# Attention for one query row: normalising at the output, score matmuls one head behind, and loads cut and ordered anew

## The chip, the cores and the metric

The kernel runs on one core of a Trainium2 chip. The metric is device microseconds of one execution. The core has five engines that run side by side and wait for each other through semaphores: TensorE (PE; its weight loads are shown as PEld), VectorE (DVE), ScalarE (ACT), GpSimd (POOL) and SyncE (SP). DMA transfers are issued by an engine's queue and carried by 16 DMA engines.

## The reference

```
batch, n_heads, kv_len, head_dim = 4, 8, 1024, 64
scores = scale * np.matmul(q, k.transpose(0, 1, 3, 2))
scores_max = np.max(scores, axis=-1, keepdims=True)
attn = np.exp(scores - scores_max) / (np.sum(np.exp(scores - scores_max), axis=-1, keepdims=True) + 1e-8)
return np.matmul(attn, v).astype(np.float32)
```

There are 32 heads (batch times heads), each with one query row of 64, and K and V of 1024 rows of 64, all float32. K and V are 8.4 MB each, so 16.8 MB are read for an output of 8 KB.

## The kernel before

**Layout.** The 1024 rows of a head are split as 128 partitions by C = 8 rows each (`p c`). [...] There are NG = 4 loads for K and 4 for V, each of HG = 8 heads: 2 MB read, 1 MB written. All eight stand first in POOL's order; the constants (`ident`, `identb`, `Wq`, `G`, `G2`; L81 to L101) are made by POOL after them. The two loads of q stand first on SP and on ACT (L72, L73).

**Scores.** q is transposed once on PE (L105) and copied by DVE into `Wq` (L110, L114), a matrix of zeros in which head h has a 64-column block with only columns 2h and 2h+1 filled. For each head, four PE transposes (L128, two rows of `c` at a time) turn K into `kt_ps` in PSUM, ACT (even heads, L135) or DVE (odd heads, L137) copies it to `kt_sb`, and a matmul (L138) with that head's block of `Wq` adds into the one accumulator `S_ps` of 64 x 512: rows 2h and 2h+1 hold the scores of head h. `kt_ps` and `kt_sb` have three buffers each.

**Softmax.** DVE takes the maximum of each row of `S_ps` (L147), ACT makes `E` = exp(scale * S - scale * m) with its row sums (L151) and `c_r` = exp(scale * m) (L159). Each head has two rows, each with its own maximum; `c_r` brings them to a common scale. `den` = `c_r` * rowsum (L160); a matmul with `G` adds the two rows of a head (L165), DVE inverts (L167), a matmul with `G2` spreads the result to both rows (L169), and `d_r` = `c_r` / Z stands on the diagonal of `dinv` (L172). Four matmuls (L177) transpose and scale `E` by it at once; DVE and ACT copy the results into `Pt` (L185, L187).

**Output.** For each head, eight matmuls (L196) of one column of `Pt` against 128 x 64 of V add into a 64-wide piece of one of four PSUM banks `avo`, eight heads to a bank. DVE and ACT copy the banks in turn into `ores` (L206, L210), and SP stores it (L211).

**What sets the order.** The program is written engine by engine by a framework that adds the semaphore waits and sets the order of each engine's instructions by its own estimate; on PE some transposes of later heads stand ahead of a head's score matmul. Pools of buffers decide when a tile may be written again. Loads issued by POOL have eight completion semaphores, used in turn.

Of the kernel before, what the change touches and what calls it, by code (L numbers as in the profile page):

```python
# [9 lines left out]

FP32 = mybir.dt.float32
BF16 = mybir.dt.bfloat16
ACT = mybir.ActivationFunctionType
ALU = mybir.AluOpType


def _strided_cols(ap: bass.AP, row0: int, nrows: int, col0: int, step: int, count: int):
    base = ap[row0 : row0 + nrows, col0 : col0 + 1]
    return bass.AP(
        tensor=base.tensor,  # L20
        offset=base.offset,
        ap=[[base.ap[0][0], nrows], [step, count]],
    )


@with_exitstack
def kernel(
# [7 lines left out]
    nc = tc.nc  # L35

    B, H, L, D = k.shape
    BH = B * H
# [4 lines left out]
    R = 2 * BH  # L43
    SCALE = 1.0 / math.sqrt(D)

    NG = 4
    HG = BH // NG

    big = ctx.enter_context(tc.tile_pool(name="big", bufs=1))
    consts = ctx.enter_context(tc.tile_pool(name="consts", bufs=1))  # L50
    small = ctx.enter_context(tc.tile_pool(name="small", bufs=1))
    ktp = ctx.enter_context(tc.tile_pool(name="ktp", bufs=3))

    k_view = k.rearrange("b h (p c) d -> p (b h) c d", c=C)
    v_view = v.rearrange("b h (p c) d -> p (b h) c d", c=C)
    q_view = q.rearrange("b h o d -> (b h) (o d)")
    out_view = out.rearrange("b h o d -> o (b h d)")

    K_bf = big.tile([P, BH, C, D], BF16, name="K_bf")
    V_bf = big.tile([P, BH, C, D], BF16, name="V_bf")  # L60
    q32 = big.tile([BH, 2, D], FP32, name="q32")
    Wq = big.tile([P, 2176], BF16, name="Wq")
    E = big.tile([R, 512], BF16, name="E")
    Pt = big.tile([P, JJ, R], BF16, name="Pt")
    ores = big.tile([1, BH * D], FP32, name="ores")

    ident = consts.tile([P, P], FP32, name="ident")
    identb = consts.tile([P, P], BF16, name="identb")
    G = consts.tile([R, BH], FP32, name="G")
    G2 = consts.tile([BH, R], FP32, name="G2")  # L70

    nc.sync.dma_start(out=q32[:, 0, :], in_=q_view)  # L72
    nc.scalar.dma_start(out=q32[:, 1, :], in_=q_view)  # L73
    for g in range(NG):
        hs = slice(g * HG, (g + 1) * HG)
        nc.gpsimd.dma_start(out=K_bf[:, hs, :, :], in_=k_view[:, hs, :, :])  # L76
    for g in range(NG):
        hs = slice(g * HG, (g + 1) * HG)
        nc.gpsimd.dma_start(out=V_bf[:, hs, :, :], in_=v_view[:, hs, :, :])  # L79

    make_identity(nc, ident[:])  # L81
    make_identity(nc, identb[:])
    nc.gpsimd.memset(Wq[:], 0.0)  # L83
    nc.gpsimd.memset(G[:], 1.0)
    nc.gpsimd.affine_select(
        out=G[:], in_=G[:], compare_op=ALU.is_ge, fill=0.0, base=0,
        channel_multiplier=1, pattern=[[-2, BH]],
    )
    nc.gpsimd.affine_select(
        out=G[:], in_=G[:], compare_op=ALU.is_ge, fill=0.0, base=1,  # L90
        channel_multiplier=-1, pattern=[[2, BH]],
    )
    nc.gpsimd.memset(G2[:], 1.0)
    nc.gpsimd.affine_select(
        out=G2[:], in_=G2[:], compare_op=ALU.is_ge, fill=0.0, base=0,
        channel_multiplier=-2, pattern=[[1, R]],
    )
    nc.gpsimd.affine_select(
        out=G2[:], in_=G2[:], compare_op=ALU.is_ge, fill=0.0, base=1,
        channel_multiplier=2, pattern=[[-1, R]],  # L100
    )  # L101

    with tc.tile_pool(name="qps", bufs=1, space=bass.MemoryType.PSUM) as qps:
        qT_ps = qps.tile([P, BH], FP32, name="qT_ps")
        nc.tensor.transpose(  # L105
            out=qT_ps[:],
            in_=q32[:].rearrange("h t d -> h (t d)"),
            identity=ident[0:BH, 0:BH],
        )
        nc.vector.tensor_copy(  # L110
            out=_strided_cols(Wq, 0, 64, 0, 66, BH),
            in_=qT_ps[0:64, :],
        )
        nc.vector.tensor_copy(  # L114
            out=_strided_cols(Wq, 64, 64, 1, 66, BH),
            in_=qT_ps[64:128, :],
        )

    c_r = small.tile([R, 1], FP32, name="c_r")
    den = small.tile([R, 1], FP32, name="den")  # L120
    with tc.tile_pool(name="ps1", bufs=1, space=bass.MemoryType.PSUM) as ps1, tc.tile_pool(
        name="ps_kt", bufs=3, space=bass.MemoryType.PSUM
    ) as ps_kt:
        S_ps = ps1.tile([R, 512], FP32, name="S_ps")
        for h in range(BH):
            kt_ps = ps_kt.tile([P, 512], BF16, name="kt_ps")
            for jj in range(JJ):
                nc.tensor.transpose(  # L128
                    out=kt_ps[:, 128 * jj : 128 * (jj + 1)],
                    in_=K_bf[:, h, 2 * jj : 2 * jj + 2, :],  # L130
                    identity=identb[:],
                )
            kt_sb = ktp.tile([P, 512], BF16, name="kt_sb")
            if h % 2 == 0:
                nc.scalar.copy(out=kt_sb[:], in_=kt_ps[:])  # L135
            else:
                nc.vector.tensor_copy(out=kt_sb[:], in_=kt_ps[:])  # L137
            nc.tensor.matmul(  # L138
                out=S_ps[:],
                lhsT=Wq[:, 64 * h : 64 * h + 64],  # L140
                rhs=kt_sb[:],
                start=(h == 0),
                stop=(h == BH - 1),
            )

        m = small.tile([R, 1], FP32, name="m")
        nc.vector.reduce_max(out=m[:], in_=S_ps[:], axis=mybir.AxisListType.X)  # L147
        negm = small.tile([R, 1], FP32, name="negm")
        nc.vector.tensor_scalar_mul(out=negm[:], in0=m[:], scalar1=-SCALE)
        rowsum = small.tile([R, 1], FP32, name="rowsum")  # L150
        nc.scalar.activation(  # L151
            out=E[:],
            in_=S_ps[:],
            func=ACT.Exp,
            bias=negm[:],
            scale=SCALE,
            accum_out=rowsum[:],
        )
    nc.scalar.activation(out=c_r[:], in_=m[:], func=ACT.Exp, scale=SCALE)  # L159
    nc.vector.tensor_mul(out=den[:], in0=c_r[:], in1=rowsum[:])  # L160

    d_r = small.tile([R, 1], FP32, name="d_r")
    with tc.tile_pool(name="ps_fix", bufs=1, space=bass.MemoryType.PSUM) as ps_fix:
        Z_ps = ps_fix.tile([BH, 1], FP32, name="Z_ps")
        nc.tensor.matmul(out=Z_ps[:], lhsT=G[:], rhs=den[:], start=True, stop=True)  # L165
        zr = small.tile([BH, 1], FP32, name="zr")
        nc.vector.reciprocal(out=zr[:], in_=Z_ps[:])  # L167
        zinv_ps = ps_fix.tile([R, 1], FP32, name="zinv_ps")
        nc.tensor.matmul(out=zinv_ps[:], lhsT=G2[:], rhs=zr[:], start=True, stop=True)  # L169
        nc.vector.tensor_mul(out=d_r[:], in0=c_r[:], in1=zinv_ps[:])  # L170
    dinv = big.tile([R, R], BF16, name="dinv")
    nc.vector.tensor_scalar_mul(out=dinv[:], in0=identb[0:R, 0:R], scalar1=d_r[:])  # L172

    with tc.tile_pool(name="ps_pt", bufs=2, space=bass.MemoryType.PSUM) as ps_pt:
        for jj in range(JJ):
            pt_ps = ps_pt.tile([P, R], FP32, name="pt_ps")
            nc.tensor.matmul(  # L177
                out=pt_ps[:],
                lhsT=E[0:R, 128 * jj : 128 * (jj + 1)],
                rhs=dinv[:],  # L180
                start=True,
                stop=True,
            )
            if jj % 2 == 0:
                nc.vector.tensor_copy(out=Pt[:, jj, :], in_=pt_ps[:])  # L185
            else:
                nc.scalar.copy(out=Pt[:, jj, :], in_=pt_ps[:])  # L187

    with tc.tile_pool(name="ps_av", bufs=1, space=bass.MemoryType.PSUM) as ps_av:
        avo = [ps_av.tile([1, 512], FP32, name=f"avo{bnk}") for bnk in range(4)]  # L190
        for h in range(BH):
            bnk = h // 8
            col = D * (h % 8)
            for c in range(C):
                t, jj = c % 2, c // 2
                nc.tensor.matmul(  # L196
                    out=avo[bnk][0:1, col : col + D],
                    lhsT=Pt[:, jj, 2 * h + t : 2 * h + t + 1],
                    rhs=V_bf[:, h, c, :],
                    start=(c == 0),  # L200
                    stop=(c == C - 1),
                )

        for bnk in range(4):
            if bnk % 2 == 0:
                nc.vector.tensor_copy(  # L206
                    out=ores[0:1, 512 * bnk : 512 * (bnk + 1)], in_=avo[bnk][:]
                )
            else:
                nc.scalar.copy(out=ores[0:1, 512 * bnk : 512 * (bnk + 1)], in_=avo[bnk][:])  # L210
    nc.sync.dma_start(out=out_view, in_=ores[:])  # L211


# [28 lines left out]
```

## Time and profile before

| | us |
|---|---|
| median of six runs | 54.53 (53.97 to 54.75) |
| profiled execution, in all | 54.5 |
| its span | 52.8 |
| first score transposes start | 11.72 |
| last score matmul starts | 34.54 |
| first `avo` matmul starts | 39.52 |
| last V load lands | 47.85 |
| output store issued | 50.55 |

The span runs from the first to the last instruction in the profile; 1.7 us lie around it. Busy shares of the span:

```profile
PE 31.4 (60%) x425; PEld 20.8 (39%) x425; DVE 10.6 (20%) x28; ACT 12.7 (24%) x24; POOL 11.0 (21%) x23
...
PE   0000000219998988988988988720449999937800
...
DVE  0000000003333233243243243162330050004000
ACT  0900000004408138138138137007030000300120
POOL 1999999992000000000000000000000000000000
PEclk9999999999999999999999999995555599999999
```

Each digit is the busy share, in tenths, of one of 40 equal slices of 1.32 us; the last row is the clock granted to TensorE in tenths of full speed.

### The profile page before, as it was taken

The numbers are of one execution on the slowest core, as the hardware profiler recorded it, in microseconds if no ns is written. First come the engines' busy times: TensorE is split into PE (matmuls) and PEld (weight loads), VectorE is DVE, ScalarE is ACT, GpSimd is POOL, SyncE is SP. The second block draws the span as 40 slices with busy tenths as digits, with TensorE's granted clock in tenths as the row PEclk, the third lists the DMA queues.
The fourth block names the chain that finished last, engine by engine and source line by source line (L and its number), as shares of the span: only waits on it lengthen the run. The fifth ranks groups of instructions, "written<-read, shape, count | busy, mean of one in ns | idle before, by whom it ended". The sixth has DMA issues, their size and how long they took to land.

```text
span 52.8 us, 1014 instructions
## 1 busy us (share of the span) xinstructions
PE 31.4 (60%) x425; PEld 20.8 (39%) x425; DVE 10.6 (20%) x28; ACT 12.7 (24%) x24; POOL 11.0 (21%) x23
## 2 busy tenths in 40 slices
PE   0000000219998988988988988720449999937800
PEld 0000000118524625625625525300329999837700
DVE  0000000003333233243243243162330050004000
ACT  0900000004408138138138137007030000300120
POOL 1999999992000000000000000000000000000000
PEclk9999999999999999999999999995555599999999
DMA  0049999999999999999999999999999999810000
GB/s 0 13 29 134 173 194 204 153 150 206 203 206 208 206 208 206 206 208 210 204 209 209 206 205 209 206 206 208 206 210 206 205 210 215 133 31 12 0 6 0
DMA packets 8421, 8.46 MB, mean 160 GB/s; under 512 B 225, under 2 KB 8417, under 8 KB 8417
## 3 DMA queue, kind: packets, MB, share of 16 engines
q0 software_dynamic: 8320, 8.39, 98.1%
q8 instruction: 3, 0.05, 0.3%
q1 hardware_dynamic: 50, 0.02, 0.1%
q10 hardware_dynamic: 48, 0.01, 0.1%
HBM read 16.79 MB, written 0.01 MB: 318 GB/s over the span
## 4 chain that ended last, share of the span: by engine, by line
DMA 76%; POOL 11%; PE 4%; issue 2%; ACT 1%; POOLq 0%
DMA V_bf<-in_v_dram 76%; POOL K_bf L76 6%; POOL V_bf L79 5%; PE avo_422 L196 4%; ACT ores L210 1%; POOLq L226 0%
## 5 line engine op out<-in xcount | busy, mean ns | idle before, releaser
L135 ACT COPY kt_sb<-kt_ps 128x512 bf16<-128x512 bf16 x16 | 8.9, 588 | 21.6 <-PE kt_ps L128 21.6
L128 PE MATMUL kt_ps<-identb,K_bf 128*128 128x128 bf16 x128 | 11.8, 232 | 2.3 <-DMA K_bf<-in_k_dram 2.2
L138 PE MATMUL S_ps<-kt_sb,Wq 128*64 128x512 bf16 x32 | 11.1, 405 | 2.3 <-ACT kt_sb L135 1.1
L137 DVE COPY kt_sb<-kt_ps 128x512 bf16<-128x512 bf16 x16 | 6.8, 425 | 27.2 <-PE kt_ps L128 26.3
L128 PEld LDWEIGHTS <-K_bf 128*128 128x128 bf16 x128 | 7.9, 103 | 10.0 <-issue 7.7
L196 PEld LDWEIGHTS <-Pt 128*1 128x1 bf16 x256 | 8.9, 90 | 1.9 <-issue 1.4
L105 PE MATMUL qT_ps<-ident,q_69 32*128 32x32 f32 x1 | 0.3, 311 | 9.2 <-POOL ident masks.py:199 9.2
L138 PEld LDWEIGHTS <-Wq 128*64 128x64 bf16 x32 | 3.1, 111 | 3.6 <-issue 1.5
L76 POOL DMA_DIRECT2D K_bf<-in_k_dram x4 | 3.7, 928 | 0.8 <-POOLq L226 0.8
L105 PEld LDWEIGHTS qT_ps<-ident,q_69 32*128 32x128 f32 x1 | 0.2, 178 | 9.2 <-POOL ident masks.py:199 9.2
L79 POOL DMA_DIRECT2D V_bf<-in_v_dram x4 | 3.5, 922 | 0.0
L196 PE MATMUL avo_419<-V_bf,Pt 128*1 128x64 bf16 x64 | 3.3, 232 | 0.3 <-ACT Pt L187 0.3
L196 PE MATMUL avo_421<-V_bf,Pt 128*1 128x64 bf16 x64 | 2.2, 193 | 0.7 <-issue 0.7
L196 PE MATMUL avo_422<-V_bf,Pt 128*1 128x64 bf16 x64 | 2.0, 193 | 0.5 <-DMA V_bf<-in_v_dram 0.5
L196 PE MATMUL avo_420<-V_bf,Pt 128*1 128x64 bf16 x64 | 2.0, 193 | 0.0
L83 POOL MEMSET Wq<- 128x2176 bf16 x1 | 2.0, 1971 | 0.0
L210 ACT COPY ores<-avo_420 1x512 f32<-1x512 f32 x1 | 0.6, 576 | 5.3 <-PE avo_420 L196 5.3
L210 ACT COPY ores<-avo_422 1x512 f32<-1x512 f32 x1 | 0.6, 575 | 4.6 <-PE avo_422 L196 4.6
L135 ACT ACT_TABLE_LOAD x1 | 1.3, 1283 | 1.3 <-PEq L226 1.3
L206 DVE COPY ores<-avo_421 1x512 f32<-1x512 f32 x1 | 0.7, 678 | 3.9 <-PE avo_421 L196 3.9
L165 PE MATMUL Z_ps<-den,G 64*32 64x1 f32 x2 | 0.2, 185 | 2.0 <-DVE den L160 2.0
L206 DVE COPY ores<-avo_419 1x512 f32<-1x512 f32 x1 | 0.7, 678 | 3.5 <-PE avo_419 L196 3.5
(32 smaller groups left out, 8.7 us busy)
## 6 DMA issues: line engine op xcount, KB each, us to landing
K_bf<-in_k_dram POOLq DMA_DIRECT2D x4, 1024.0 KB, 16.7
V_bf<-in_v_dram POOLq DMA_DIRECT2D x4, 1024.0 KB, 33.4
q_69<-in_q_dram ACTq DMA_DIRECT2D x1, 8.0 KB, 1.8
q_69<-in_q_dram SPq DMA_DIRECT2D x1, 8.0 KB, 1.7
out_dram<-ores SPq DMA_DIRECT2D x1, 8.0 KB
```

The lines of the kernel that those rows point to most:

```text
L76: nc.gpsimd.dma_start(out=K_bf[:, hs, :, :], in_=k_view[:, hs, :, :])
L79: nc.gpsimd.dma_start(out=V_bf[:, hs, :, :], in_=v_view[:, hs, :, :])
L83: nc.gpsimd.memset(Wq[:], 0.0)
L105: nc.tensor.transpose(out=qT_ps[:], in_=q32[:].rearrange("h t d -> h (t d)"), identity=ident[0:BH, 0:BH],)
L128: nc.tensor.transpose(out=kt_ps[:, 128 * jj : 128 * (jj + 1)], in_=K_bf[:, h, 2 * jj : 2 * jj + 2, :], identity=identb[:],)
L135: nc.scalar.copy(out=kt_sb[:], in_=kt_ps[:])
L137: nc.vector.tensor_copy(out=kt_sb[:], in_=kt_ps[:])
L138: nc.tensor.matmul(out=S_ps[:], lhsT=Wq[:, 64 * h : 64 * h + 64], rhs=kt_sb[:], start=(h == 0), stop=(h == BH - 1),)
L165: nc.tensor.matmul(out=Z_ps[:], lhsT=G[:], rhs=den[:], start=True, stop=True)
L196: nc.tensor.matmul(out=avo[bnk][0:1, col : col + D], lhsT=Pt[:, jj, 2 * h + t : 2 * h + t + 1], rhs=V_bf[:, h, c, :], start=(c == 0), stop ...
L206: nc.vector.tensor_copy(out=ores[0:1, 512 * bnk : 512 * (bnk + 1)], in_=avo[bnk][:])
L210: nc.scalar.copy(out=ores[0:1, 512 * bnk : 512 * (bnk + 1)], in_=avo[bnk][:])
```

## The change

K is loaded in eight groups of four heads; V in five groups of 8, 8, 6, 6 and 4 heads. On POOL the first K group is issued before the constants, the second and third between the selects of `G`, and the others after them. The fills with constants move from POOL to DVE, so that POOL keeps the selects only; `G2` is gone. `kt_ps` and `kt_sb` have four buffers, and the loop emits the score matmul of a head after the transposes of the next. `c_r` is made ahead of `E`, and `dinv` holds `c_r` alone, so that the transposed weights are not normalised. The sums of the heads are added, inverted and transposed into one row `zinv_row` after the transposed weights are made and ahead of the `avo` matmuls, and DVE multiplies each bank by it when it copies it to `ores`; ACT copies no bank any more.

In the built program, the order of POOL is: first K group; selects of `ident`, `identb` and `G`; second K group; second select of `G`; six K groups; five V groups. The first V group waits for the first K group to have landed, the second for the second, and so on to the fifth.

```diff
@@ -5,7 +5,6 @@
 import concourse.bass as bass
 import concourse.tile as tile
 from concourse import bass_utils, mybir
-from concourse.masks import make_identity
 from concourse._compat import with_exitstack
 
 FP32 = mybir.dt.float32
@@ -20,6 +19,23 @@
         tensor=base.tensor,
         offset=base.offset,
         ap=[[base.ap[0][0], nrows], [step, count]],
+    )
+
+
+def _bcast_last(ap2d: bass.AP, n: int):
+    return bass.AP(
+        tensor=ap2d.tensor,
+        offset=ap2d.offset,
+        ap=[ap2d.ap[0], ap2d.ap[1], [0, n]],
+    )
+
+
+def _build_identity(nc, ident: bass.AP):
+    sq = ident.shape[0]
+    nc.vector.memset(ident, 0.0)
+    nc.gpsimd.affine_select(
+        out=ident, in_=ident, compare_op=ALU.not_equal, fill=1.0, base=0,
+        pattern=[[-1, sq]], channel_multiplier=1,
     )
 
 
@@ -43,13 +59,14 @@
     R = 2 * BH
     SCALE = 1.0 / math.sqrt(D)
 
-    NG = 4
-    HG = BH // NG
+    KG = 4
+    VGROUPS = [8, 8, 6, 6, 4]
+    assert sum(VGROUPS) == BH and BH % KG == 0
 
     big = ctx.enter_context(tc.tile_pool(name="big", bufs=1))
     consts = ctx.enter_context(tc.tile_pool(name="consts", bufs=1))
     small = ctx.enter_context(tc.tile_pool(name="small", bufs=1))
-    ktp = ctx.enter_context(tc.tile_pool(name="ktp", bufs=3))
+    ktp = ctx.enter_context(tc.tile_pool(name="ktp", bufs=4))
 
     k_view = k.rearrange("b h (p c) d -> p (b h) c d", c=C)
     v_view = v.rearrange("b h (p c) d -> p (b h) c d", c=C)
@@ -63,25 +80,24 @@
     E = big.tile([R, 512], BF16, name="E")
     Pt = big.tile([P, JJ, R], BF16, name="Pt")
     ores = big.tile([1, BH * D], FP32, name="ores")
+    zinv_row = big.tile([1, BH], FP32, name="zinv_row")
 
     ident = consts.tile([P, P], FP32, name="ident")
     identb = consts.tile([P, P], BF16, name="identb")
     G = consts.tile([R, BH], FP32, name="G")
-    G2 = consts.tile([BH, R], FP32, name="G2")
-
-    nc.sync.dma_start(out=q32[:, 0, :], in_=q_view)
-    nc.scalar.dma_start(out=q32[:, 1, :], in_=q_view)
-    for g in range(NG):
-        hs = slice(g * HG, (g + 1) * HG)
-        nc.gpsimd.dma_start(out=K_bf[:, hs, :, :], in_=k_view[:, hs, :, :])
-    for g in range(NG):
-        hs = slice(g * HG, (g + 1) * HG)
-        nc.gpsimd.dma_start(out=V_bf[:, hs, :, :], in_=v_view[:, hs, :, :])
-
-    make_identity(nc, ident[:])
-    make_identity(nc, identb[:])
-    nc.gpsimd.memset(Wq[:], 0.0)
-    nc.gpsimd.memset(G[:], 1.0)
+
+    def issue_k(h0, h1):
+        nc.gpsimd.dma_start(out=K_bf[:, h0:h1, :, :], in_=k_view[:, h0:h1, :, :])
+
+    def issue_v(h0, h1):
+        nc.gpsimd.dma_start(out=V_bf[:, h0:h1, :, :], in_=v_view[:, h0:h1, :, :])
+
+    issue_k(0, KG)
+
+    _build_identity(nc, ident[:])
+    _build_identity(nc, identb[:])
+    nc.vector.memset(Wq[:], 0.0)
+    nc.vector.memset(G[:], 1.0)
     nc.gpsimd.affine_select(
         out=G[:], in_=G[:], compare_op=ALU.is_ge, fill=0.0, base=0,
         channel_multiplier=1, pattern=[[-2, BH]],
@@ -90,15 +106,16 @@
         out=G[:], in_=G[:], compare_op=ALU.is_ge, fill=0.0, base=1,
         channel_multiplier=-1, pattern=[[2, BH]],
     )
-    nc.gpsimd.memset(G2[:], 1.0)
-    nc.gpsimd.affine_select(
-        out=G2[:], in_=G2[:], compare_op=ALU.is_ge, fill=0.0, base=0,
-        channel_multiplier=-2, pattern=[[1, R]],
-    )
-    nc.gpsimd.affine_select(
-        out=G2[:], in_=G2[:], compare_op=ALU.is_ge, fill=0.0, base=1,
-        channel_multiplier=2, pattern=[[-1, R]],
-    )
+
+    nc.sync.dma_start(out=q32[:, 0, :], in_=q_view)
+    nc.scalar.dma_start(out=q32[:, 1, :], in_=q_view)
+
+    for h0 in range(KG, BH, KG):
+        issue_k(h0, h0 + KG)
+    h0 = 0
+    for n in VGROUPS:
+        issue_v(h0, h0 + n)
+        h0 += n
 
     with tc.tile_pool(name="qps", bufs=1, space=bass.MemoryType.PSUM) as qps:
         qT_ps = qps.tile([P, BH], FP32, name="qT_ps")
@@ -119,10 +136,11 @@
     c_r = small.tile([R, 1], FP32, name="c_r")
     den = small.tile([R, 1], FP32, name="den")
     with tc.tile_pool(name="ps1", bufs=1, space=bass.MemoryType.PSUM) as ps1, tc.tile_pool(
-        name="ps_kt", bufs=3, space=bass.MemoryType.PSUM
+        name="ps_kt", bufs=4, space=bass.MemoryType.PSUM
     ) as ps_kt:
         S_ps = ps1.tile([R, 512], FP32, name="S_ps")
-        for h in range(BH):
+
+        def transposes(h):
             kt_ps = ps_kt.tile([P, 512], BF16, name="kt_ps")
             for jj in range(JJ):
                 nc.tensor.transpose(
@@ -135,6 +153,9 @@
                 nc.scalar.copy(out=kt_sb[:], in_=kt_ps[:])
             else:
                 nc.vector.tensor_copy(out=kt_sb[:], in_=kt_ps[:])
+            return kt_sb
+
+        def score_mm(h, kt_sb):
             nc.tensor.matmul(
                 out=S_ps[:],
                 lhsT=Wq[:, 64 * h : 64 * h + 64],
@@ -143,10 +164,19 @@
                 stop=(h == BH - 1),
             )
 
+        prev = None
+        for h in range(BH):
+            kt_sb = transposes(h)
+            if prev is not None:
+                score_mm(*prev)
+            prev = (h, kt_sb)
+        score_mm(*prev)
+
         m = small.tile([R, 1], FP32, name="m")
         nc.vector.reduce_max(out=m[:], in_=S_ps[:], axis=mybir.AxisListType.X)
         negm = small.tile([R, 1], FP32, name="negm")
         nc.vector.tensor_scalar_mul(out=negm[:], in0=m[:], scalar1=-SCALE)
+        nc.scalar.activation(out=c_r[:], in_=m[:], func=ACT.Exp, scale=SCALE)
         rowsum = small.tile([R, 1], FP32, name="rowsum")
         nc.scalar.activation(
             out=E[:],
@@ -156,20 +186,9 @@
             scale=SCALE,
             accum_out=rowsum[:],
         )
-    nc.scalar.activation(out=c_r[:], in_=m[:], func=ACT.Exp, scale=SCALE)
+    dinv = big.tile([R, R], BF16, name="dinv")
+    nc.vector.tensor_scalar_mul(out=dinv[:], in0=identb[0:R, 0:R], scalar1=c_r[:])
     nc.vector.tensor_mul(out=den[:], in0=c_r[:], in1=rowsum[:])
-
-    d_r = small.tile([R, 1], FP32, name="d_r")
-    with tc.tile_pool(name="ps_fix", bufs=1, space=bass.MemoryType.PSUM) as ps_fix:
-        Z_ps = ps_fix.tile([BH, 1], FP32, name="Z_ps")
-        nc.tensor.matmul(out=Z_ps[:], lhsT=G[:], rhs=den[:], start=True, stop=True)
-        zr = small.tile([BH, 1], FP32, name="zr")
-        nc.vector.reciprocal(out=zr[:], in_=Z_ps[:])
-        zinv_ps = ps_fix.tile([R, 1], FP32, name="zinv_ps")
-        nc.tensor.matmul(out=zinv_ps[:], lhsT=G2[:], rhs=zr[:], start=True, stop=True)
-        nc.vector.tensor_mul(out=d_r[:], in0=c_r[:], in1=zinv_ps[:])
-    dinv = big.tile([R, R], BF16, name="dinv")
-    nc.vector.tensor_scalar_mul(out=dinv[:], in0=identb[0:R, 0:R], scalar1=d_r[:])
 
     with tc.tile_pool(name="ps_pt", bufs=2, space=bass.MemoryType.PSUM) as ps_pt:
         for jj in range(JJ):
@@ -186,6 +205,15 @@
             else:
                 nc.scalar.copy(out=Pt[:, jj, :], in_=pt_ps[:])
 
+    with tc.tile_pool(name="ps_z", bufs=1, space=bass.MemoryType.PSUM) as ps_z:
+        Z_ps = ps_z.tile([BH, 1], FP32, name="Z_ps")
+        nc.tensor.matmul(out=Z_ps[:], lhsT=G[:], rhs=den[:], start=True, stop=True)
+        zr = small.tile([BH, 1], FP32, name="zr")
+        nc.vector.reciprocal(out=zr[:], in_=Z_ps[:])
+        zT_ps = ps_z.tile([1, BH], FP32, name="zT_ps")
+        nc.tensor.transpose(out=zT_ps[:], in_=zr[:], identity=ident[0:BH, 0:BH])
+        nc.vector.tensor_copy(out=zinv_row[:], in_=zT_ps[:])
+
     with tc.tile_pool(name="ps_av", bufs=1, space=bass.MemoryType.PSUM) as ps_av:
         avo = [ps_av.tile([1, 512], FP32, name=f"avo{bnk}") for bnk in range(4)]
         for h in range(BH):
@@ -202,12 +230,12 @@
                 )
 
         for bnk in range(4):
-            if bnk % 2 == 0:
-                nc.vector.tensor_copy(
-                    out=ores[0:1, 512 * bnk : 512 * (bnk + 1)], in_=avo[bnk][:]
-                )
-            else:
-                nc.scalar.copy(out=ores[0:1, 512 * bnk : 512 * (bnk + 1)], in_=avo[bnk][:])
+            ores_v = ores[0:1, 512 * bnk : 512 * (bnk + 1)].rearrange(
+                "o (h d) -> o h d", d=D
+            )
+            avo_v = avo[bnk][:].rearrange("o (h d) -> o h d", d=D)
+            zb = _bcast_last(zinv_row[0:1, 8 * bnk : 8 * (bnk + 1)], D)
+            nc.vector.tensor_tensor(out=ores_v, in0=avo_v, in1=zb, op=ALU.mult)
     nc.sync.dma_start(out=out_view, in_=ores[:])
 
 
```

## The prediction

> **What bounds the kernel now.** I read the chain of waits first, because it says which work ended last, in order of time:
>
> ```profile
> 4.95 2.60 POOL V_bf L79 x3
> 7.55 40.30 DMA V_bf<-in_v_dram
> 47.85 0.04 issue
> 47.89 2.04 PE avo_422 L196 x64
> 49.93 0.02 issue
> 49.95 0.57 ACT ores L210
> ```
>
> The columns are start, length and what. The last V load is issued at 7.55 us and lands at 47.85; everything after that is a tail: 64 matmuls (2.04), one copy (0.57), and the output transfer, which with the end of the program fills the rest to 52.79 (2.27 after 50.52). So the end is: landing of the last V group plus 4.94 us. What sets that landing is the DMA stream:
>
> ```profile
> DMA  0049999999999999999999999999999999810000
> GB/s 0 13 29 134 173 194 204 153 150 206 203 206 208 206 208 206 206 208 210 204 209 209 206 205 209 206 206 208 206 210 206 205 210 215 133 31 12 0 6 0
> ```
>
> One slice is 1.32 us. The engines are full from the fourth slice until about 45 us; nothing downstream holds the stream back, since all eight loads are issued at the start. There are three places where it is less than perfect: the ramp, a dip in slices 7 and 8, and the end, where the rate falls to 133, 31, 12 while a straggling engine finishes. Busy time by stretch (length, PE, PEld, DVE, ACT, POOL, granted clock, DMA share, GB/s) prices the first two:
>
> ```profile
> 3.00:8.50 5.50, 0.00 (x0) 0.00 (x0) 0.00 (x0) 0.00 (x0) 5.50 (x8) 1.00 1.06 150
> 8.50:10.00 1.50, 0.31 (x1) 0.18 (x1) 0.00 (x0) 0.00 (x0) 1.50 (x5) 1.00 1.21 194
> 10.00:11.50 1.50, 0.00 (x0) 0.00 (x0) 0.00 (x0) 0.00 (x0) 1.50 (x4) 1.00 0.95 120
> 11.50:27.00 15.50, 14.07 (x110) 7.79 (x110) 5.17 (x13) 6.16 (x11) 0.64 (x4) 1.00 1.24 207
> ```
>
> Against 207 GB/s the first row loses 5.5 x 57/207 = 1.5 us, the third 1.5 x 87/207 = 0.63 us. In the first POOL is issuing the loads; in the third it is filling Wq. Landing times:
>
> ```profile
> K_bf<-in_k_dram POOLq DMA_DIRECT2D x4, 1024.0 KB, 16.7
> V_bf<-in_v_dram POOLq DMA_DIRECT2D x4, 1024.0 KB, 33.4
> ```
>
> The first K group lands at 11.7 (the transposes start then); the answer for K_bf has 22.9 us as its longest flight, which from the fourth issue at about 4.1 is 27.0. From there to 47.85 four V groups land, 5.2 us each, or 0.65 us a head. PE finishes the scores at 34.9 (last L138 at 34.54 plus 0.38), eight microseconds after the last K: its period in the timeline is 3.98 us for six heads, 0.66 a head, from a late start at 11.7. It starts on V at 39.5 and is still just in time, since it finishes avo_421 at 47.38 and only then waits 0.5 for the last landing.
>
> **The change part by part.**
>
> *Last V group of 4 heads, not 8.* On the path. 64 matmuls cost 2.04; spacing from first to last start is (49.73 - 47.89)/63 = 29 ns. 32 of them: 31 x 29 + 193 = 1.10 us, if the clock is full. But the same group at half clock, avo_419, had
>
> ```profile
> 39.52 3.27 PE L196 MATMUL avo_419<-V_bf,Pt 128*1 128x64 bf16 x64 [0.30 <-ACT Pt L187]
> 42.63 2.03 PE L196 MATMUL avo_420<-V_bf,Pt 128*1 128x64 bf16 x64
> ```
>
> (42.63 - 39.52)/64 = 49 ns each, so 32 take 31 x 49 + 241 = 1.75. Which clock? The clock row has 5 in slices 28 to 31, about 35.5 to 42.3, one drop of some 6.8 us. Ahead of it the PE was not idle for long: from 32.1 to 35.5 it ran four matmuls of L138 and some eight transposes. At the full-clock pace (ten 128-column transposes take 0.73 us with the latency of 0.22, a 512-column L138 holds PE for about 0.21) that is some 1.3 us of 3.4, under 40%. [...] After the change PE will do bursts of 1.4 us (six heads, 48 x 29 ns) every 3.9 us (six heads x 0.65), with gaps of 2.5. [...] The row is the measurement, but the fill is so near to it that I take the middle, 1.42: a gain of 0.62 (0.29 to 0.94).
>
> *The end on DVE with a multiply.* ACT copied the last bank in 0.575; DVE's copy of the same shape, L206, takes 0.678. The multiply reads a second, tiny operand; not in the trace, so from 0.58 (no dearer than ACT) to about 1.35 (twice the copy, if the second operand halved the rate). I take 0.68, the nearest row: +0.10. Banks 0 to 2 are behind the stream, as their copies are now.
>
> *Thirteen loads for eight.* Eight K loads of 4 heads and five V loads (8, 8, 6, 6, 4) replace four and four: 13 against 8, the same bytes. [...] I take the trace: 5 x 0.02 = +0.1 for the extra ends, 0 to 0.65 (5 x 0.13).
>
> *Who issues when.* POOL now does: K0, three selects, K1, one select, six K, five V. The first selects wait for DVE's fills. DVE starts beside ACT and SP at about 0.8: two fills, then Wq as 1088 words, then G. POOL took 1.97 for Wq; DVE's nearest row, 512 elements in 0.678, makes it about 1.3, so G is ready near 2.5. K0's issue begins at 1.32 as now; a whole group takes 0.92 of POOL, so K0 ends between 1.8 (half) and 2.3 (all of it fixed). Selects follow at their present pitch of 0.25, K1 is issued near 3.0. K0's own 0.5 MB needs 2.6 us or more of stream from about 3, so K1 comes in time; that cover fails only if K1 is some 2 us later. The remaining K loads take at most 0.92 each against 2.6 us of transfer. The V loads wait, in the built order, for the landing of K0, K1, K2, K3 and K4; behind each wait on POOL there are only further V loads. V4 is thus issued near 3 + 5 x 2.6 = 16 us, with K5 to K7 and V0 to V3 still queued (some 26 us of work): cost nothing. The q loads are written later in the program but stand first on SP and on ACT, ahead of the table load, and wait for nothing: nothing.
>
> *What this does to the landing.* Data now begins near 3.1, 1.8 us after the first issue; if it needs the whole instruction to be generated, half the size brings 0.46; if not, 0. The Wq fill leaves POOL: if it made the dip, 0.63; if not, 0. The loss of 1.5 while POOL generates could go up or down with the loads' generating time; see the second rival. I take roughly half of the first two, 0.55, less the 0.1: last landing at 47.4, 0.45 earlier (1.1 earlier to 1.3 later).
>
> *Score matmuls one head behind, four buffers; normalisation moved.* Off the path. Scores can start when K0 lands, near 7 instead of 11.7. In the built order each score matmul now stands about two heads of transposes behind its own, so the waits for the copies (1.1 for ACT, 0.6 for DVE) and some issue gaps go; the rate is then the stream's 0.65 a head. Scores end about 2.5 after the last K, near 29.5. From there to the first avo matmul were 4.6 us; the two G steps between E and the transposed weights (den at 36.66 to d_r's end at 38.05) leave, 1.4, and return in part as Z, reciprocal, transpose ahead of avo in PE's order, about 0.9. So V work starts near 34, and V0 (landed near 32) costs 2.0 to 3.1: PE catches up with the stream at V1 (near 37). All of this is worth nothing at the end, where the stream decides; cover lacks only if V work starts after about 38.
>
> *Sum.* 52.79 - 0.45 - 0.62 + 0.10 = 51.82. The profiled execution has 54.5 in all, 1.71 outside its span, and agrees with the median, 54.53. 51.82 + 1.71 = **53.5 us**.
>
> **The rivals.**
>
> *Nothing, within a measurement's reach.* The last landing stays at 47.85 and the last burst runs at half clock: 52.79 - 0.29 + 0.10 + 1.71 = 54.3. For it: the rate of 207 is flat for 33 us and no edit touches it. Against: the dip fits the Wq fill in time.
>
> *Slower: generating the loads drags the stream for longer.* In the trace the rate is 150 while POOL generates (seven microseconds, 8 x 0.92), 207 afterwards. If POOL's time per load is mostly fixed, 13 x 0.92 = 12 us are generated, 4.7 more, at a loss of 57/207: +1.3. Then 52.79 + 1.3 - 0.62 + 0.10 + 1.71 = 55.3. It cancels the tail's gain from 0.5 us of loss, that is 1.9 us more generating; it is over 1% slower from 3.9 more. Against: the first microseconds are a ramp in any case, and 8.5 to 10 shows 194 with POOL busy at something else.
>
> *Everything comes.* Landing 1.1 earlier, full clock: 52.79 - 1.1 - 0.94 + 0.10 + 1.71 = 52.6.
>
> *That the change doesn't do what it says.* The old order already ran transposes ahead of score matmuls (the timeline has nine or ten in a row), so the pipelining may be a small shift; it moves no number above, because the scores are not on the path.
>
> **How the numbers follow.** Forecast 0.50, everything 0.17, nothing 0.21, slower 0.12. A measurement here can tell about 1% from no change: 53.98 to 55.08. Faster: forecast but for a little, everything, and a bit of the nothing case, 0.70; within 1%, 0.18; slower, 0.12. The range leaves out the slower case and the far end of the best: 52.5 to 54.5.
>
> **What would show it.** Right: the chain ends in a V load, 32 matmuls and a DVE row; scores end near 30 and PE shows gaps between V groups; a last landing near 47.4. The clock in the last burst decides 1.10 against 1.75. The rate between 10 and 11.5 says whether the Wq fill made the dip; the rate while V0 to V4 are issued says whether generating costs. Wrong: a gap in the DMA row before K1, a V load issued after its turn in the stream, or PE still at avo when the last group lands.

## The result and the profile after

The changed kernel takes 53.54 us (median of 8 runs, 53.05 to 54.17) against 54.52 before: ratio 0.9801, 95% interval 0.976 to 0.9842. The profiled execution took 53.24, with a span of 51.5 against 52.8. Some executions run disturbed and a per cent or more longer; the ratios leave them out and the medians do not, so that a median and a ratio can seem not to fit. The forecast time, 53.5, was met; two of the terms that make it were not, and they cancelled.

The end of the chain of waits of the changed kernel, in order of time (start, length, what):

```profile
4.60 11.28 DMA K_bf<-in_k_dram
15.88 0.28 issue
16.16 0.82 POOL V_bf L93
16.98 1.70 issue
18.68 0.02 POOLq L265
18.70 27.93 DMA V_bf<-in_v_dram
46.64 0.04 issue
46.68 1.88 PE avo_423 L224 x32
48.56 0.02 issue
48.58 0.68 DVE ores L238
```

The row at 4.60 is the fourth K load; its landing at 15.88 releases V's fourth issue, and V's fifth, at 18.70, waits in the same way for the fifth K load. Then come 27.9 us of flight. The wait until 18.7 is no loss: by estimate the load is queued 25 us before its data flow, as its 0.5 MB at 207 GB/s take the last 2.5 us before 46.64. (Of the K loads, POOL's timeline has the second at 2.92, between the two selects of `G`, and the other six from 3.85 on, after both.)

Two numbers are to be compared with before. The last landing is at 46.64, 1.21 earlier. The last burst has half the matmuls, yet takes 1.88 against 2.04. The multiply takes 0.68 where ACT's copy took 0.57. So 1.21 + 0.16 - 0.11 = 1.26, and the spans differ by 52.79 - 51.51 = 1.28.

The profile's rows for PE, the clock and the stream, in slices of 1.29 us (the first is slice 0):

```profile
PE   0020069879899999999999950459999750777600
...
PEclk9999999999999999999999997555569999955555
DMA  0039999999999999999999999999999999930000
GB/s 0 13 49 188 181 153 186 161 202 204 208 204 205 206 209 200 207 216 200 203 209 205 209 206 208 206 208 207 206 208 212 201 207 204 208 66 0 0 6 0
```

PE is at work from slice 5 (first transposes at 6.84 us, before 11.72), the scores end 4.5 us sooner (30.41), and V work starts at 34.39 (before 39.52). Late in the kernel PE shows gaps, as it now waits for the third, fourth and fifth V group (0.27, 2.24 and 0.67 us), and from 45.2 us on the granted clock is 0.50. The stream still dips twice, at slices 5 and 7 (153 and 161 GB/s), but is a little ahead.

### The profile page after: what moved, and what is told of

Read it like the earlier page. It is cut to its first block, busy times and chain, and to the rows that moved or that the text cites. A ratio compares the mean times of both kernels' runs of the same rounds, so it can differ in the third digit from the quotient of the medians.

```text
span 51.5 us, 1012 instructions
## 1 busy us (share of the span) xinstructions
PE 35.0 (68%) x424; PEld 22.7 (44%) x424; DVE 13.3 (26%) x34; ACT 12.0 (23%) x22; POOL 11.3 (22%) x21
## 4 chain that ended last, share of the span: by engine, by line
DMA 76%; POOL 6%; issue 5%; DVE 4%; PE 4%; POOLq 0%
DMA V_bf<-in_v_dram 54%; DMA K_bf<-in_k_dram 22%; PE avo_423 L224 4%; POOL K_bf L90 3%; DVE Wq L99 2%; POOL V_bf L93 2%; DVE ores L238 1%; POOL ident L36 1%; POOL identb L36 0%; POOL G L105 0%; DVE ident L35 0%; POOL G L101 0%; DVE identb L35 0%; POOLq L265 0%; DVE G L100 0%
## 5 line engine op out<-in xcount | busy, mean ns | idle before, releaser
L146 PE MATMUL kt_ps<-identb,K_bf 128*128 128x128 bf16 x128 | 13.3, 235 | 4.6 <-DMA K_bf<-in_k_dram 4.6
L153 ACT COPY kt_sb<-kt_ps 128x512 bf16<-128x512 bf16 x16 | 9.4, 585 | 17.6 <-PE kt_ps L146 17.6
L159 PE MATMUL S_ps<-kt_sb,Wq 128*64 128x512 bf16 x32 | 13.1, 423 | 0.1
L224 PEld LDWEIGHTS <-Pt 128*1 128x1 bf16 x256 | 10.5, 96 | 3.8 <-issue 3.8
L90 POOL DMA_DIRECT2D K_bf<-in_k_dram x8 | 6.1, 779 | 0.8 <-POOLq L254 0.8
L93 POOL DMA_DIRECT2D V_bf<-in_v_dram x5 | 4.2, 842 | 7.0 <-DMA K_bf<-in_k_dram 7.0
L224 PE MATMUL avo_422<-V_bf,Pt 128*1 128x64 bf16 x64 | 2.2, 193 | 2.5 <-DMA V_bf<-in_v_dram 2.5
L224 PE MATMUL avo_420<-V_bf,Pt 128*1 128x64 bf16 x64 | 3.6, 241 | 0.3 <-DVE zinv_row L215 0.3
L224 PE MATMUL avo_423<-V_bf,Pt 128*1 128x64 bf16 x64 | 3.3, 226 | 0.7 <-DMA V_bf<-in_v_dram 0.7
L224 PE MATMUL avo_421<-V_bf,Pt 128*1 128x64 bf16 x64 | 2.3, 201 | 0.0
L196 PE MATMUL pt_ps<-dinv,E 64*128 64x64 bf16 x4 | 0.5, 228 | 2.1 <-ACT E L181 1.8
L238 DVE TENSOR_TENSOR ores<-avo_422,zinv_row 1x512 f32<-1x512 f32 x1 | 0.7, 678 | 4.0 <-PE avo_422 L224 4.0
L238 DVE TENSOR_TENSOR ores<-avo_420,zinv_row 1x512 f32<-1x512 f32 x1 | 0.7, 678 | 3.7 <-PE avo_420 L224 3.7
L238 DVE TENSOR_TENSOR ores<-avo_423,zinv_row 1x512 f32<-1x512 f32 x1 | 0.7, 679 | 3.1 <-PE avo_423 L224 3.1
L238 DVE TENSOR_TENSOR ores<-avo_421,zinv_row 1x512 f32<-1x512 f32 x1 | 0.7, 678 | 1.4 <-PE avo_421 L224 1.4
## 6 DMA issues: line engine op xcount, KB each, us to landing
V_bf<-in_v_dram POOLq DMA_DIRECT2D x1, 512.0 KB, 27.9
```

Of the source, the lines that this page charges most:

```text
L90: nc.gpsimd.dma_start(out=K_bf[:, h0:h1, :, :], in_=k_view[:, h0:h1, :, :])
L93: nc.gpsimd.dma_start(out=V_bf[:, h0:h1, :, :], in_=v_view[:, h0:h1, :, :])
L146: nc.tensor.transpose(out=kt_ps[:, 128 * jj : 128 * (jj + 1)], in_=K_bf[:, h, 2 * jj : 2 * jj + 2, :], identity=identb[:],)
L159: nc.tensor.matmul(out=S_ps[:], lhsT=Wq[:, 64 * h : 64 * h + 64], rhs=kt_sb[:], start=(h == 0), stop=(h == BH - 1),)
L196: nc.tensor.matmul(out=pt_ps[:], lhsT=E[0:R, 128 * jj : 128 * (jj + 1)], rhs=dinv[:], start=True, stop=True,)
L224: nc.tensor.matmul(out=avo[bnk][0:1, col : col + D], lhsT=Pt[:, jj, 2 * h + t : 2 * h + t + 1], rhs=V_bf[:, h, c, :], start=(c == 0), stop ...
```

## The experiments

All times are medians, and each ratio is against the kernel before, measured beside it on the same chip. The quicker kernels scatter more from run to run than the kernel before does.

**e1, the fill alone.** In the kernel before, one line:

```diff
-    nc.gpsimd.memset(Wq[:], 0.0)
+    nc.vector.memset(Wq[:], 0.0)
```

> The kernel before with one line changed: the fill of Wq is made by DVE instead of POOL. Theory A (the POOL fill made the dip to 120 GB/s at 10 to 11.5 us): the rate there rises to about 200, all later landings come about 0.6 us earlier, and the time is about 53.9 us. Theory B (the dip belongs to the first change from one load to the next): the dip stays and the time is 54.5, as before.

54.52 us, ratio 0.9982 (0.9949 to 1.0015). The stretch from 10 to 11.5 us (length, PE, PEld, DVE, ACT, POOL, clock, DMA share, GB/s):

```profile
10.00:11.50 1.50, 0.00 (x0) 0.00 (x0) 0.13 (x1) 0.00 (x0) 0.24 (x2) 1.00 1.04 130
```

POOL is all but idle there now (0.24 us busy), and the rate is 130, where it was 120. Theory A falls: the dip is not made by the fill. The end of this profile shows something more: its chain ends in PE, without a landing.

```profile
39.87 6.70 PE avo L196 x180
46.57 0.50 issue
47.07 2.49 PE avo L196 x76
```

So in nearly the kernel before, PE on V can be the last limit as well as the landing.

**e2, the cut of V alone.** In the kernel before, V in groups of 8, 8, 6, 6 and 4 heads:

```diff
-    for g in range(NG):
-        hs = slice(g * HG, (g + 1) * HG)
-        nc.gpsimd.dma_start(out=V_bf[:, hs, :, :], in_=v_view[:, hs, :, :])
+    h0 = 0
+    for n in [8, 8, 6, 6]:
+        nc.gpsimd.dma_start(out=V_bf[:, h0 : h0 + n, :, :], in_=v_view[:, h0 : h0 + n, :, :])
+        h0 += n
...
+    nc.gpsimd.dma_start(out=V_bf[:, 28:32, :, :], in_=v_view[:, 28:32, :, :])
```

> The kernel before with V in groups of 8, 8, 6, 6 and 4 heads; the fifth is issued after the fills on POOL. Everything else as before. If the last burst of 32 instead of 64 matmuls is worth its size at full clock, 0.9 us less: 53.6. If the clock has dropped by then, 0.3 less or nothing: 54.2 to 54.5. The last landing should stay near 47.8.

54.45 us, ratio 0.996 (0.9925 to 0.9995): almost nothing, though the clock in its runs was the one of before (mean 0.935). e7 shows why.

**e3, everything but the cut of V.** In the changed kernel:

```diff
-    VGROUPS = [8, 8, 6, 6, 4]
+    VGROUPS = [8, 8, 8, 8]
```

> The changed kernel with V in four groups of 8. If the split is what brings the time: back to about 54.3 (0.8 slower than the changed kernel). If the bursts of 64 keep the clock full, the tail is 2.0 us instead of 1.9 and the time is 53.6, the split worth next to nothing.

54.81 us, ratio 1.0002 (0.9966 to 1.0038). Without the cut nothing is left of the gain. Its last burst:

```profile
46.83 0.04 issue
46.87 3.31 PE avo L224 x64
```

Its landing, 46.83, is a microsecond ahead of before; 64 matmuls at 3.31 us instead of 2.04 give that microsecond back. The landing was earlier and the tail longer: in this profile the early landing buys nothing, because the last burst runs at half clock (0.51 granted from 47.2 to 50.6 us).

**e4, the loads alone.** The order of loads and constants of the changed kernel (with `G2` made beside `G`), and all of the compute of the kernel before:

```diff
-    NG = 4
-    HG = BH // NG
+    KG = 4
+    VGROUPS = [8, 8, 6, 6, 4]
...
+    issue_k(0, KG)
...
+    for h0 in range(KG, BH, KG):
+        issue_k(h0, h0 + KG)
+    h0 = 0
+    for n in VGROUPS:
+        issue_v(h0, h0 + n)
+        h0 += n
```

> The load and constant order of the changed kernel with all of the compute of the kernel before: score matmuls as before with three buffers, normalisation between E and the transposed weights, banks copied by DVE and ACT. If the compute changes are worth nothing at the end: 53.5, as the changed kernel. If the earlier start on V matters (PE late, or another clock in the last burst): 54 or more.

52.84 us, ratio 0.9649 (0.96 to 0.9698). The loads by themselves bring all of the gain; the compute changes do not add to it.

```profile
18.30 28.24 DMA V_bf<-in_v_dram
46.55 0.04 issue
46.59 1.11 PE avo L214 x32
47.70 0.02 issue
47.72 0.57 ACT ores L228
```

The landing is where the changed kernel has it (46.55 against 46.64). What differs in the span is the burst, 1.11 against 1.88, and the copy, 0.57 against 0.68.

**e5, PE kept busy.** The changed kernel, with seven matmuls into an unused bank ahead of head 22 and two ahead of head 28:

```diff
+        spare = ps_av.tile([64, 512], FP32, name="spare")
         for h in range(BH):
+            for _ in range({22: 7, 28: 2}.get(h, 0)):
+                nc.tensor.matmul(
+                    out=spare[:], lhsT=identb[:, 0:64],
+                    rhs=K_bf[:, 0, :, :].rearrange("p c d -> p (c d)"),
+                    start=True, stop=True,
+                )
```

> The changed kernel with nine more matmuls of 128x64 by 128x512 into an unused PSUM bank: seven ahead of head 22 and two ahead of head 28, where PE waits for V. They add work and nothing else. Theory A (the changed kernel loses 0.8 us to the kernel with its loads alone because PE, early on V, pauses between groups and has lost its clock by the last burst): the last burst takes 1.1 us instead of 1.9 and the time is 52.7 to 52.9. Theory B (the loss is in the work itself: the multiply, the order of the softmax): 53.5 or a little more.

52.74 us, ratio 0.9688 (0.9631 to 0.9744), and the burst:

```profile
46.71 1.11 PE avo L231 x32
47.82 0.02 issue
47.84 0.68 DVE ores L245
```

More work, and no slower: faster than the first measurement of the changed kernel (0.9801), and not to be told from the second (0.9719 in e11, below). The multiply and the order of the softmax are those of the changed kernel, and the burst takes 1.11, so Theory B falls for the burst.

**e6, the old score loop in the changed kernel.**

```diff
-            kt_sb = transposes(h)
-            if prev is not None:
-                score_mm(*prev)
-            prev = (h, kt_sb)
-        score_mm(*prev)
+            score_mm(h, transposes(h))
```

and three buffers instead of four.

> The changed kernel with the score loop of before: each score matmul straight after its own transposes, three buffers. If the lead of the scores only makes PE earlier on V and the clock is what it costs: scores end about 1.4 us later, as with the loads alone, and the time lies between 52.8 and 53.5, the clock steadier from run to run. If the lead is worth anything on the path: slower than 53.5.

53.15 us, with runs from 52.31 to 53.97; ratio 0.9684 (0.9589 to 0.9779). It lies between, as expected, but the scatter is as large as what was to be told apart. It shows no loss from taking the lead of the scores away.

**e7, K in large loads.** In the loads-alone kernel:

```diff
-    KG = 4
+    KG = 8
```

> The loads-alone kernel with K in four groups of 8, everything else as there. Theory A (the stream starts better because the first load is half as large): the lead of about 0.15 to 0.19 MB over the kernel before at 11 us is gone, the last landing is near 47.4 and the time 53.6. Theory B (the order, constants between the loads and fewer loads generated while the stream starts, brings it): the lead stays and the time is 52.8.

54.99 us, ratio 1.0042 (0.9993 to 1.009). Its end, by the chain and with `avo` in 32 heads times 8:

```profile
39.70 6.79 PE avo L214 x180
46.48 0.39 issue
46.87 2.39 PE avo L214 x76
49.28 0.57 ACT ores L228
```

From the first K load's landing at 11.59 on, no DMA is in the chain. PE starts on V at 39.70 and works without a wait for V until 49.26; the last V group is there before PE wants it. The dip near 10 us is back as well (132 GB/s from 10 to 11.5): from 3 to 11 us the stream moved 154 GB/s in e7, 152 in the kernel before, 173 in e4:

```profile
3.00:11.00 8.00, 0.08 (x1) 0.00 (x0) 0.59 (x2) 0.00 (x0) 6.66 (x11) 1.00 1.10 154
```

```profile
3.00:11.00 8.00, 3.62 (x21) 2.11 (x21) 1.41 (x4) 1.17 (x2) 6.95 (x12) 1.00 1.14 173
```

(e7 first, e4 second; the same columns as above.) Other profiles agree: 152 to 154 in the kernel before, e1 and e7, with K in large loads, 160 to 174 in the changed kernel, e4, e5, e6, e8, e11 and e12, with small ones. So the lead in the stream comes from small K loads, and not from what stands between the loads in POOL's order. And with large K loads the cut of V is worth nothing, because PE is then the later of the two limits, in e7 as in e2, where its work on V goes from 40.74 to 50.63 without a wait.

**e8, a smaller end.** The loads-alone kernel with V in 8, 8, 6, 6, 2 and 2 heads, and five banks of 8, 8, 8, 6 and 2 heads, the last copied by DVE (in e4 by ACT):

```diff
-    VGROUPS = [8, 8, 6, 6, 4]
+    VGROUPS = [8, 8, 6, 6, 2, 2]
...
+        firsts = [0, 8, 16, 24, 30, 32]
```

> The loads-alone kernel with the last 4 heads of V loaded as two groups of 2, and the last 2 heads in a PSUM tile of their own, so that the last burst has 16 matmuls and the last copy 128 elements. If the tail is only its own work: burst 0.6 instead of 1.1, copy about 0.3 instead of 0.6, the landing unmoved: 52.0. If the clock is lost ahead of the last burst or small loads delay the landing: 52.6 or more.

52.12 us, ratio 0.9533 (0.9466 to 0.9599), the fastest of all:

```profile
47.14 0.04 issue
47.18 0.64 PE avo L218 x16
47.82 0.02 issue
47.84 0.28 DVE ores L229
```

Burst and copy are 0.92 us together, against 1.68 in e4. This profiled execution landed 0.6 later than e4's, with a slower start of the stream (162 GB/s from 3 to 11 us), so its span, 50.4, hides part of it.

Not all of the lead over e4 is this shorter end. The time less the span is 2.1 to 2.3 us in every run of e4, e7, e9 and e12, and 1.7 to 1.8 in e8; in the changed kernel it is 1.7 to 1.85. Over the runs that the ratios count, e8's median span is 50.2 against 50.5 in e4: 0.3 of the 0.7 us between their times lie inside the span, 0.4 outside. What these 0.4 us are stays open. They also make e4, e7, e9 and e12 look about that much slower against the kernel before than by their spans.

**e9, only the first and the last K load small**, and **e10, a still smaller start**:

```diff
-    KG = 4
+    KGROUPS = [4, 8, 8, 8, 4]
```

```diff
-    KG = 4
+    KGROUPS = [2, 2, 4, 4, 4, 8, 8]
```

> The loads-alone kernel with K in groups of 4, 8, 8, 8 and 4. Theory A (only the first load's size matters: the stream starts sooner and PE starts on K near 7 us): the lead of 0.15 to 0.19 MB at 11 us is there, V work starts near 36 to 37, the time is 52.8 to 53.1. Theory B (all K loads must be small, so that PE follows the stream and ends its scores soon after the last of them): V work starts at 38 or later and the time is 53.6 or more.

> The small-end kernel with K in groups of 2, 2, 4, 4, 4, 8 and 8. If the ramp is set by how long the first load takes POOL to generate: data starts up to 0.2 us sooner, the last landing comes that much sooner, 51.9. If two heads are too little to cover the selects and the generating of the next load: a gap in the stream near 4 us and 52.3 or more.

e9: 54.52 us, ratio 0.9966 (0.992 to 1.0012). In its profile, of the slowest of its twelve runs, PE starts at 7.25, but then waits 3.27 us for the second load, and V work starts at 40.5. Theory B's forecast came: a small first and a small last K load are not enough. (Over the runs that the ratio counts its span is about 0.5 us under that of the kernel before; the time outside the span takes most of that back.) e10, on the small end: 53.78 us (52.68 to 55.34, too scattered for a ratio). In its profile, of the quickest of its six runs, the first load lands at 5.0, yet V work starts at 38.45, where e8 has 35.9. Its last two K loads are large, and PE sets the end again:

```profile
38.45 7.19 PE avo L220 x180
45.65 0.17 issue
45.81 2.39 PE avo L220 x76
```

The signs of both answers in its expectation came: data flow sooner (156 GB/s from 3.4 to 3.8 us, 59 in e8), then the stream has a gap (41 GB/s from 4.6 to 5.0, 195 in e8), and the time is over 52.3. But what set the end is neither of them; that PE would be late on V, the expectation did not name.

**e11, the changed kernel again.**

> The changed kernel once more, unaltered, to see how its last burst and its clock vary: 53.5 with mean granted clocks between 0.87 and 0.96 from run to run, where the loads-alone kernel had 0.926 to 0.933.

53.02 us, ratio 0.9719 (0.9649 to 0.9788), clocks 0.877 to 0.964. The clocks scatter as expected, and this profiled execution kept the full clock to the end (1.00 granted from 45.49 to 48.90):

```profile
46.51 0.04 issue
46.55 1.11 PE avo L224 x32
```

The same program, the same landing within 0.13, a burst of 1.11 instead of 1.88, a span of 50.6 instead of 51.5. So the changed kernel has two ends, and two executions of it showed one each. That this makes its scatter is not shown: the mean clock does not order its times (53.41 us at 0.951, 53.24 at 0.872). The landing scatters as much: over the eight profiles with small K loads it lies between 46.51 and 47.21. The two measurements of the kernel, 0.9801 and 0.9719, are the scatter of the whole.

**e12, the new score loop on the loads-alone kernel**, with four buffers.

```diff
+        prev = None
+        for h in range(BH):
+            kt_sb = transposes(h)
+            if prev is not None:
+                score_mm(*prev)
+            prev = (h, kt_sb)
+        score_mm(*prev)
```

> The loads-alone kernel with the score loop of the changed kernel (score matmuls one head behind, four buffers), the normalisation still between E and the transposed weights. Theory A (an earlier start on V lengthens PE's pause ahead of the third V group, and with it the risk to the clock): V work starts near 34.5 instead of 35.8, the mean granted clock varies from run to run as in the changed kernel, and the time is 53.0 to 53.5. Theory B (it was the normalisation at the output): 52.8 with a steady clock.

53.71 us, ratio 0.9821 (0.973 to 0.9913), clocks 0.918 to 0.955: the scatter of Theory A, and a time a little over its 53.0 to 53.5. But V work started at 35.60, as late as without the new loop (35.77), and the burst took 1.11, as in e4 at a granted clock of 1.00; the time lay in a landing at 47.12 and in the time outside the span. So it is no proof of A's way. Which of the compute changes goes with the half clock of the last burst stays open.

## Why the prediction was right, and where it was wrong

**The tail decides, and the cut of V is what shortens it: right.** e3 without the cut is at 1.0002, and with both at half clock its last burst takes 3.31 against 1.88. The cut alone brings nothing (e2, e7), for the reason under "K's loads" below.

**The clock of the last burst: mis-sized.** The prediction took 1.42 us, the middle between full clock (1.10) and half (1.75), because its bursts would fill about as much of the time as a stretch of the kernel before that had lost the clock. That this share decides was its own estimate, and no run shows the 1.42, or the gain of 0.62 worked out from it. An execution gets one or the other: 1.11 in e11 and 1.88 in the first profile, the latter at 52 ns from start to start, dearer than the 49 taken for the bound of 1.75. In the kernel before the granted clock falls to half at 35.48 us, is full again from 42.31 and falls at 52.55; in the changed kernel it falls at 31.54, is full again from 38.37 and falls at 45.19. The steps are 6.83 and 10.24, then 6.83 and 6.83: two and three times 3.41. The rows take stretches of about that length, first of the changed kernel, the second of them up to where its clock fell, then of e11:

```profile
38.40:41.80 3.40, 3.13 (x104) 3.02 (x102) 0.96 (x2) 0.00 (x0) 0.00 (x0) 1.00 1.24 207
41.80:45.20 3.40, 1.16 (x41) 1.06 (x37) 0.39 (x1) 0.00 (x0) 0.00 (x0) 1.00 1.23 204
45.20:48.60 3.40, 2.68 (x50) 2.36 (x45) 0.30 (x2) 0.00 (x0) 0.00 (x0) 0.50 0.11 20
```

```profile
38.66:42.07 3.41, 3.41 (x119) 3.40 (x116) 1.36 (x2) 0.00 (x0) 0.00 (x0) 1.00 1.24 208
42.07:45.49 3.42, 1.58 (x52) 1.45 (x48) 0.68 (x1) 0.00 (x0) 0.00 (x0) 1.00 1.09 181
45.49:48.90 3.41, 1.18 (x35) 0.95 (x31) 0.68 (x1) 0.00 (x0) 0.00 (x0) 1.00 0.04 7
```

PE was busy for 1.16 of 3.40 us (34%) and the clock fell at the stretch's end, from 1.00 to 0.50; with 1.58 of 3.42 (46%) it stayed at 1.00. In e3 the stretch before the burst had 0.55 of 3.40, and it fell to 0.51. The longest pause of PE among the V groups of the changed kernel was 2.24 us.

Yet the busy share is not what sorts the stretches. Here is the one ahead of the drop in the kernel before (0.50 from 35.48 to 42.30), and one of e4 after which the clock stayed full (1.00 from 46.48 to 49.89):

```profile
32.07:35.48 3.41, 2.03 (x14) 0.77 (x11) 1.38 (x3) 0.96 (x2) 0.00 (x0) 1.00 1.24 207
43.06:46.48 3.42, 1.56 (x48) 1.45 (x48) 0.68 (x1) 0.00 (x0) 0.00 (x0) 1.00 0.79 132
```

60% lost the clock, 46% kept it. What does sort them is how many columns PE was given: 64 for an `avo` matmul, 128 for a score transpose, 512 for a score matmul. Counted by the matmuls that start in each stretch of 3.41 us (the x in the rows counts those running over from the stretch before as well), from 15.0 us on in the trace of the kernel before and from 11.1 on in that of the changed kernel, the four full-clock stretches with at most 2816 columns were followed by half clock, and the thirteen with at least 4160 were not; the stretches of e4 and e11 with 3072, in the rows above, were not either. This is a count over these stretches, not an experiment made for it. Six heads are 48 matmuls, 3072 columns: in one stretch, as in e4 and e11, the clock stayed. In the changed kernel the fourth V group's work began at 44.14 and the clock fell at 45.19, after 37 matmuls (2368 columns); in e11 it began at 44.01, and all 48 started before 45.49, the end of the stretch in its row. So the size of the burst was read rightly; what differed between these two executions of one program is how many of its matmuls came before the end of a stretch. e5 fills the pause, and its burst had the full clock (1.11 us, 1.00 granted).

**The last landing: mis-sized.** Forecast 47.4, measured 46.64. The reasons given were half wrong. The fill of Wq was given part of a possible 0.63; e1 shows it is worth none. The earlier first data was given part of 0.46; e9, with a small first load, has such a start too (195 and 187 GB/s from 4.2 to 5.0 us in steps of 0.4, before 143 and 92) and loses it again between 7 and 12 us (148 GB/s from 3 to 11 us, 152 in the kernel before). What counted is that the K loads behind the first are small as well (e4 against e7 and e9). Why the stream dips early on, and less with small K loads, is not shown by any run. The landing was better than forecast by 0.76 and the burst worse by 0.46, which leaves the span 0.3 under the forecast of 51.8; the profiled execution is likewise 0.3 under the median of the runs, so that the median meets the forecast. That the sum came out is luck: two errors of opposite sign.

**K's loads and the scores, "worth nothing at the end": wrong for the loads.** This is the step that failed without showing in the total. The kernel before had two limits close together: the last landing at 47.85, and PE, done with `avo_421` at 47.38. With the last burst's 2 us behind it, PE alone would have ended only half a microsecond sooner; in e1's profile it is PE that ends last. A shorter last group or an earlier landing is therefore worth little unless PE comes to V sooner, and that is what small K loads bring: V work from 35.8 in e4 against 39.7 in e7. The prediction had the threshold ("only if V work starts after about 38") but counted the early start as cover and not as part of the gain; e2, e7, e9 and e10, all above 38 in their profiles, show its price, up to all of the gain in e2, e7 and e9. (In e7 and e9 part of that price lies outside the span, as told under e8.) For the lead of the scores and the normalisation, "worth nothing" holds: e4 does without them and is no slower. V work did start near 34 (34.39), but PE first waited for V at 40.34, for the third group, and not near 37 for the second: the first group, at half clock (0.50 granted from 31.54 to 38.37), took 3.4 us and not 2.0 to 3.1.

**The multiply: right.** 0.678 and 0.679, as DVE's copy (0.678).

**Thirteen loads for eight: right to follow the trace.** The prediction took 0.1 us for the five extra loads; no run shows the 0.02 a load that it is made of. What the traces show is this: in the kernel before, groups of 1 MB land 5.2 us apart, and 1 MB at the measured 207 GB/s is 5.07; in the changed kernel the stream kept 206 GB/s while four of V's loads were generated:

```profile
10.90:19.50 8.60, 8.41 (x66) 4.22 (x64) 2.55 (x6) 3.51 (x6) 3.27 (x4) 1.00 1.24 206
```

**The slower rival: its premise was right, its mechanism fell.** POOL's time per load is indeed mostly fixed: 0.78 us for 4 heads of K, against 0.93 for 8. POOL thus spends 10.3 us on loads (6.1 + 4.2) against 7.2, 3.1 more. But the row above shows full rate while POOL works on loads for 3.27 of 8.60 us, and from 3 to 11 us the stream with small K loads is quicker, not slower. What generating costs at the very start of the stream was not separated.

## What to carry to other kernels

Where two limits end within a microsecond of each other, undoing one shows only the other: cut the first input's loads small enough that the consumer starts early, and the last input's so that little work is left behind its landing, and do both: either alone brought nothing here. Then look at the clock in the last burst: in the changed kernel PE had caught up with its loads, paused for up to 2.24 us and did its last burst in 1.88 us at half clock (0.50); with nine spare matmuls in the pauses it had the full clock in e5 (1.11), and in e4, which starts on V later (35.77 against 34.39), as well (1.11). Of this change, the loads alone with a last group of 2 heads were the best, at 0.9533.

## What the runs showed that was not expected

POOL's issue of a load of K cost nearly the same for half the size (0.78 against 0.93 us), and with the stream under way it took nothing from it (206 GB/s). In the changed kernel the clock was lost with no pause of PE among the V groups above 2.24 us. Not PE's busy share sorts the stretches that lost it (60% lost it, 46% kept it) but, as far as the count above goes, the columns given to PE (at most 2816 lost it, 3072 and more kept it). And the last load landed only when the stream had all but run dry: in the kernel before, the DMA row falls from 8 tenths of the 16 engines to 1 tenth, and the rate over 133, 31 and 12 GB/s, before the last landing; in the changed kernel's profile the rate falls to 66 and then to nothing, in e11 over 131 and 15. So a part of the 1.21 us of earlier landing is a shorter trail and not an earlier stream. What shortens it was not tried.
